# Product-key queries in one pass over four token tiles, or in two passes over pairs with the scatter between them

## The chip, the cores and the metric

One core of a Trainium2 chip runs the whole program. The metric is device microseconds (us) of one execution; lower is better.

## What is computed

One layer: differential attention and an HGRN2 recurrence share an input and an output projection, then a product-key expert layer (PEER) runs on 512 tokens. The change touches the expert layer alone:

```python
def peer_ffn(h, w_query, subkeys, u_table, v_table):      # h: 512 tokens x 1024, blocks of 128
    def one_block(xb):
        q = jnp.einsum('nd,dc->nc', xb, w_query).reshape(PEER_BLOCK, PEER_HEADS, 2, PEER_QUERY_DIM // 2)
        s = jnp.einsum('nhpc,hpkc->nhpk', q, subkeys)       # 8 heads x 2 halves x 128 keys
        sv, si = lax.top_k(s, PEER_TOPK)                    # 16 of 128
        cand_s = sv[:, :, 0, :, None] + sv[:, :, 1, None, :]
        cand_i = si[:, :, 0, :, None] * N_KEYS + si[:, :, 1, None, :]
        top_s, pos = lax.top_k(cand_s, PEER_TOPK)           # 16 of 256 pairs
        experts = jnp.take_along_axis(cand_i, pos, axis=-1)
        gates = jax.nn.softmax(top_s, axis=-1)
        hid = gelu(jnp.einsum('nkd,nd->nk', u_table[experts], xb)) * gates
        return jnp.einsum('nk,nkd->nd', hid, v_table[experts])
```

There are 16384 experts, and each token uses 8 x 16 of them.

## The kernel before

The 512 tokens are four tiles of 128. Three of them (0, 1 and 2, `ND` = 3) are computed densely: for every one of 128 groups of 128 experts, h = gelu(u x) for all 384 tokens, times a table of gates that is zero wherever a token did not choose the expert, then y += h v. The fourth tile (`SP`, tile 3) gathers its own rows of u and v with indirect DMAs.

Products are made of three matmuls each (`mm3`, lines 111 to 113) on a high and a low part of both operands. `split` makes the parts: ScalarE copies the high part (line 107), VectorE or, where `G` is given, GpSimd subtracts it for the low part (line 108). `u_piece` (lines 662 to 668) loads a piece of 128 x 1024 on SP's queue (line 664) and splits it; it has three buffers each for the raw piece `ur` and its parts `uh` and `ul`, which the query weights `wq` share with the pieces of u.

The stages, in the order of the program:

1. Projections, recurrence, attention and the output projection, until 333 us. None of it changes.
2. Queries. A loop over 16 sets (8 heads x 2 halves): 24 matmuls of the set's `wq` with all 512 tokens into `ps_q`, a copy by ScalarE, four matmuls with the keys into `pss` (line 771), then the top 16 of each tile's 128 scores on VectorE (`top16`: two `max`, two `max_index` and a `match_replace`, lines 752 to 756). After every second set GpSimd adds the 54 candidate pairs of a head for four tiles (line 779, five instructions), and VectorE takes the top 16 of each.
3. Softmax of all tiles at once (lines 878 to 895), then `route(0)` (lines 797 to 852), a chain of VectorE operations that turns list positions into expert numbers, then `scatter` (lines 897 to 914): tile 0's gates are added into a zeroed table in HBM (`g_dram[0]`, in the order listings `g_dram_61`) by 8 heads x 16 indirect DMAs from GpSimd (line 904). A head waits until all DMAs of the head before it have landed, since two heads may name the same expert.
4. Gates of tiles 1 and 2. `gates4` (lines 854 to 874) builds one-hot rows `oh` on VectorE, multiplies them on TensorE into `pgt`, and ScalarE copies them to `stg`; SP writes `stg` to `g_dram[1]` and `g_dram[2]` (line 934).
5. Last stage (from line 1008): for each of 128 groups i, SP loads the gates `gsl` (line 1021, after the scatter) and v's piece `vr` (line 1029), and TensorE runs 18 matmuls `y`, then the h piece that refills the ring. GpSimd's gathers for tile 3 (`ug`, line 953) run beside it.

While VectorE and GpSimd route and scatter, TensorE has the h pieces: `run_ahead(n)` takes n steps of the first 40 (`RING`), a piece being 24 matmuls `ps_h` of 384 columns in four steps (`h_parts`, lines 696 to 710). Once 40 are done there is no buffer for another until `y` uses one up; only the loads and splits of piece 40 are issued ahead (`h_load`, line 939), with its low part on GpSimd.

The tile framework's scheduler orders each engine's instructions from the order in the code and its own estimates. GpSimd and SP run in order, so what waits at the head of either holds all behind it.

Of the kernel before, what the change touches and what calls it, by code (L numbers as in the profile page):

```python
# [20 lines left out]
P = 128  # L21
# [40 lines left out]
def tile_kernel(  # L62
# [653 lines left out]
    with ExitStack() as rt:  # L716
        rc = rt.enter_context(tc.tile_pool(name="rc", bufs=1))
        qs = rt.enter_context(ExitStack())
# [31 lines left out]
        def top16(vals, n, vdst, idst):  # L750
            t = rw.tile([P, n], F32, name="t16", tag=f"t16_{n}")
            V.max(vdst[:, 0:8], vals)
            V.max_index(idst[:, 0:8], vdst[:, 0:8], vals)
            V.match_replace(out=t, in_to_replace=vdst[:, 0:8], in_values=vals, imm_value=FMIN)
            V.max(vdst[:, 8:16], t)
            V.max_index(idst[:, 8:16], vdst[:, 8:16], t)

        for s in range(NSET):
            wh, wl = u_piece(wq[s], G) if s else qw_first
            ps = pq.tile([P, SEQ], F32, name="ps_q", tag="pq")  # L760
            parts = [slice(0, 256), slice(256, SEQ)] if s == 0 else [slice(0, SEQ)]
            for part in parts:
                if part.start:
                    s3(SP, X.pop(SP), pg, "pg")
                for kc in range(KC):
                    mm3(ps[:, part], wh[:, kc], wl[:, kc], xbh[:, kc, part], xbl[:, kc, part], kc == 0, kc == KC - 1)
            qT = rw.tile([P, SEQ], F32, name="qT")
            S.activation(qT, ps, AF.Copy)
            pss = pg.tile([P, NTB, NK], F32, name="pss", tag="pg")
            for tb in range(NTB):  # L770
                PE.matmul(pss[:, tb, :], qT[:, tb * P : tb * P + P], skt[:, s, :], start=True, stop=True)
            for tb in range(NTB):
                top16(pss[:, tb, :], NK, SV[tb][:, s, :], SI[tb][:, s, :])
            if s % 2 == 1:
                hh = s // 2
                cand = rw.tile([P, NTB, NCAND], F32, name="cand")
                o = 0
                for a0, na, nb in CBLK:
                    G.tensor_tensor(
                        cand[:, :, o : o + na * nb].rearrange("p t (a b) -> p t a b", b=nb),  # L780
                        SVA[:, :, s - 1, a0 : a0 + na].unsqueeze(3).to_broadcast([P, NTB, na, nb]),
                        SVA[:, :, s, :nb].unsqueeze(2).to_broadcast([P, NTB, na, nb]),
                        op=OP.add,
                    )
                    o += na * nb
                for tb in range(NTB):
                    top16(cand[:, tb], NCAND, TS[tb][:, hh, :], TI[tb][:, hh, :])

        qs.close()
        rw = rt.enter_context(tc.tile_pool(name="rg", bufs=2, reuse_waits="tile"))  # L790
        steps = (None for i in range(RING) for _ in h_parts(i, None, HP))

        def run_ahead(n):
            for _ in range(n):
                next(steps, None)

        def route(tb):
# [3 lines left out]
            def pick(which, sel, op, key, table, dt):  # L801

                eq = rw.tile([P, PH * TOPK, TOPK], dt, name="eq", tag="eq", bufs=1)
# [7 lines left out]
                ix = rw.tile([P, PH, TOPK], U32 if dt == I16 else F32, name=f"ix{which}")  # L811
                V.tensor_tensor(ix.rearrange("p h k -> p (h k)"), eq[:, :, 0], eq[:, :, 1], op=OP.add)
                return ix
# [3 lines left out]
            comb = rw.tile([P, PH, TOPK], I16, name="comb", bufs=1)  # L817
            step = rw.tile([P, PH, TOPK], I16, name="step", bufs=1)
# [6 lines left out]
            k1 = rw.tile([P, PH, TOPK], U32, name="k1", bufs=1)  # L825
            V.tensor_scalar(k1, both, 6, None, op0=OP.logical_shift_right)
            V.tensor_scalar(both, both, 63, None, op0=OP.bitwise_and)
            ixa = rw.tile([P, PH, TOPK], F32, name="ixa")
            V.tensor_copy(ixa, k1)
            rank = rw.tile([P, PH, TOPK], F16, name="rank", bufs=1)  # L830
            V.tensor_tensor(rank, TI[tb], both, op=OP.subtract)
            sif = rw.tile([P, PH, TOPK], F16, name="sif", bufs=1)
# [15 lines left out]
            for i, t in enumerate((idx[0], idx[1], gh[:, tb], TS[tb])):  # L848
                PE.transpose(ptp[:, i, :], t.rearrange("p h k -> p (h k)"), ident)
            pmj = rw.tile([P, 4, P], F16, name="pmj")  # L850
# [25 lines left out]
        run_ahead(16)  # L876

        fl = "p t h k -> p (t h) k"
        mx = rc.tile([P, NTB * PH], F32, name="mx")
        V.tensor_copy(mx, TSA[:, :, :, 0].rearrange("p t h -> p (t h)"))  # L880
        g3 = TSA.rearrange(fl)
        V.tensor_tensor(g3, g3, mx.unsqueeze(2).to_broadcast([P, NTB * PH, TOPK]), op=OP.subtract)
        tc.keep_in_program_order(S.activation(g3, g3, AF.Exp))
        V.tensor_reduce(mx, g3, axis=AX.X, op=OP.add)
        V.reciprocal(mx, mx)
        V.tensor_tensor(g3, g3, mx.unsqueeze(2).to_broadcast([P, NTB * PH, TOPK]), op=OP.mult)
        V.tensor_copy(exp_g, TS[SP].rearrange("p h k -> p (h k)"))
        sc_g = rc.tile([P, PH, TOPK], F32, name="sc_g")
        V.tensor_scalar(sc_g, TS[0], GS, None, op0=OP.mult)
        gh16 = rw.tile([P, ND, PH, TOPK], F16, name="gh16", bufs=1)  # L890
        gh = rw.tile([P, ND, PH, TOPK], F32, name="gh", bufs=1)
        V.tensor_scalar(TSA[:, :ND], TSA[:, :ND], GS, None, op0=OP.mult)
        V.tensor_copy(gh16, TSA[:, :ND])
        V.tensor_copy(gh, gh16)
        V.tensor_tensor(TSA[:, :ND], TSA[:, :ND], gh, op=OP.subtract)

        def scatter(sc_idx):
# [24 lines left out]
        run_ahead(16)  # L922
        acc_ = 0.0
        for tb in range(1, ND):
            pmj = nxt
            for g0 in range(0, P, GB):
# [196 lines left out]
```

## Time and profile before

| | us |
|---|---|
| median of three runs (lowest, highest) | 1693.4 (1690.3, 1697.65) |
| the profiled execution, whole | 1696.98 |
| its span (first to last instruction) | 1695.2 |
| TensorE busy | 1559.5 (92% of the span) |
| VectorE / ScalarE / GpSimd busy | 1197.9 / 642.1 / 683.7 |
| granted TensorE clock, mean | 0.962 |

The profile is of one execution. An engine's busy share is an average over the stages; what bounds a stage is read from that stretch of time: which engine has no idle time there, or what the others wait for. Times in the rows count from the start of the span, which is 1.8 us shorter than the execution's own time.

### The profile page before, as it was taken

The page shows a single profiled execution, that of the slowest core. Times are in us where ns is not written, and L with a number is a line of the kernel's source. Part 1 is how long each engine was busy: PE and PEld are TensorE (multiplying, and loading weights), DVE is VectorE, ACT ScalarE, POOL GpSimd, SP SyncE. Part 2 cuts the span into 40 slices and gives each one's busy share as a digit, 9 for nine tenths or more (in the row PEclk, how much of TensorE's full clock was granted, in tenths as well). Part 3 has the DMA queues.
Part 4 walks back from the last instruction along what each step waited for, and adds up shares of the span by engine and source line. Part 5 has one row for each costly group of instructions (what it writes and reads, how often), then busy time and mean ns, then how long its engine had stood idle before and what let it go on. Part 6 is the DMA issues. An engine that isn't in the chain of part 4 may idle for free.

```text
span 1695.2 us, 23411 instructions
## 1 busy us (share of the span) xinstructions
PE 1559.5 (92%) x8599; PEld 1397.2 (82%) x8599; DVE 1197.9 (71%) x2354; ACT 642.1 (38%) x984; POOL 683.7 (40%) x522
## 2 busy tenths in 40 slices
PE   8999999999699999305999999999999999999997
PEld 7999977788698999204999999999999999998885
DVE  7762667578988877003888777777777787767775
ACT  5223364422256666101333333333333333333333
POOL 3000012334138886874544444444444444433221
PEclk9999999999899999656999999999999999999999
DMA  8511321322144666227999998899899888977883
GB/s 284 190 51 56 108 96 67 131 94 73 57 121 112 199 186 188 1 0 277 342 348 308 321 329 306 306 321 329 307 315 316 321 311 303 337 234 253 285 268 137
DMA packets 166948, 364.00 MB, mean 215 GB/s; under 512 B 31152, under 2 KB 80560, under 8 KB 166704
## 3 DMA queue, kind: packets, MB, share of 16 engines
q1 hardware_dynamic: 110816, 227.11, 38.5%
q0 software_dynamic: 55440, 134.34, 25.4%
q8 instruction: 67, 1.10, 0.2%
q10 hardware_dynamic: 576, 1.05, 0.2%
q14 instruction: 49, 0.40, 0.1%
HBM read 330.92 MB, written 29.43 MB: 213 GB/s over the span
## 4 chain that ended last, share of the span: by engine, by line
PE 70%; POOL 13%; DVE 7%; issue 4%; DMA 3%; ACT 2%; SPq 1%; POOLq 0%; DVEq 0%; ACTq 0%
POOL g_dram L904 12%; PE y L112 10%; PE y L113 10%; PE y L111 10%; PE ps_h L113 7%; PE ps_h L111 7%; PE ps_h L112 7%; DMA g_dram<-sc_g,sc_idx 2%; PE ps_l L351 2%; PE ps_t L113 2%; PE ps_t L111 2%; PE ps_t L112 2%; PE ps_n L111 1%; PE ps_n L112 1%; PE ps_n L113 1%
## 5 line engine op out<-in xcount | busy, mean ns | idle before, releaser
L113 PE MATMUL ps_h<-xbh,ul 128*128 128x384 f32 x1024 | 347.1, 339 | 94.4 <-POOL ul L108 82.1
L111 PE MATMUL ps_h<-xbh,uh 128*128 128x384 f32 x1024 | 350.2, 342 | 1.3 <-ACT hr L707 1.3
L112 PE MATMUL ps_h<-xbl,uh 128*128 128x384 f32 x1024 | 345.8, 338 | 0.0
L111 PE MATMUL y<-vh,wh 128*128 128x512 f32 x768 | 300.2, 391 | 9.9 <-ACT wh L107 9.8
L108 DVE TENSOR_TENSOR vl<-vr,vh 128x1024 fp32r<-128x1024 f32 x128 | 156.8, 1225 | 205.5 <-ACT vh L107 203.8
L112 PE MATMUL y<-vl,wh 128*128 128x512 f32 x768 | 301.6, 393 | 0.0
L113 PE MATMUL y<-vh,wl 128*128 128x512 f32 x768 | 301.6, 393 | 0.0
L967 POOL DMA_INDIRECT vg<-in_v_dram,exp_idx x128 | 186.1, 1454 | 278.0 <-DVE acc L973 208.8
L113 PEld LDWEIGHTS ps_h<-xbh,ul 128*128 128x128 f32 x1024 | 194.2, 190 | 95.8 <-POOL ul L108 82.4
L953 POOL DMA_INDIRECT ug<-in_u_dram,exp_idx x128 | 179.2, 1400 | 216.7 <-DVE jk L957 137.2
L904 POOL DMA_INDIRECT g_dram<-sc_g,sc_idx x128 | 222.4, 1737 | 84.4 <-issue 38.8
L107 ACT ACTIVATE uh<-ur 128x1024 fp32r<-128x1024 f32 x144 | 152.8, 1063 | 267.6 <-PE ps_h L112 175.9
L107 ACT ACTIVATE vh<-vr 128x1024 fp32r<-128x1024 f32 x128 | 136.1, 1063 | 270.4 <-issue 214.8
L111 PEld LDWEIGHTS ps_h<-xbh,uh 128*128 128x128 f32 x1024 | 195.3, 191 | 5.1 <-ACT hr L707 1.5
L112 PEld LDWEIGHTS ps_h<-xbl,uh 128*128 128x128 f32 x1024 | 194.5, 190 | 3.4
L111 PEld LDWEIGHTS y<-vh,wh 128*128 128x128 f32 x768 | 144.9, 189 | 38.9 <-ACT wh L107 10.6
L113 PEld LDWEIGHTS y<-vh,wl 128*128 128x128 f32 x768 | 144.8, 189 | 30.5
L112 PEld LDWEIGHTS y<-vl,wh 128*128 128x128 f32 x768 | 144.8, 189 | 28.6
L973 DVE SCALAR_TENSOR_TENSOR acc<-vg,hid,acc 128x1024 f32<-128x1024 f32 x127 | 162.8, 1282 | 2.1
L108 DVE TENSOR_TENSOR ul<-ur,uh 128x1024 fp32r<-128x1024 f32 x127 | 155.0, 1221 | 7.9 <-ACT uh L107 7.8
L957 DVE SCALAR_TENSOR_TENSOR jk<-ug,xbn 128x1024 f32<-128x1024 f32 x128 | 156.4, 1222 | 4.8 <-DMA ug<-in_u_dram,exp_idx 2.3
L107 ACT ACTIVATE wh<-hr 128x384 fp32r<-128x384 f32 x128 | 67.3, 525 | 226.1 <-DVE hr L1034 226.1
(274 smaller groups left out, 2503.8 us busy)
## 6 DMA issues: line engine op xcount, KB each, us to landing
ur<-in_uT_dram SPq DMA_DIRECT2D x128, 512.0 KB
vr<-in_v_dram SPq DMA_DIRECT2D x128, 512.0 KB
gsl<-g_dram SPq DMA_DIRECT2D x96, 256.0 KB
g_dram<-stg SPq DMA_DIRECT2D x32, 512.0 KB
wr<-in_w_in_dram SPq DMA_DIRECT2D x26, 512.0 KB
g_dram<-zero SPq DMA_DIRECT2D x4, 2048.0 KB
ur<-in_wq_dram SPq DMA_DIRECT2D x16, 512.0 KB
wor<-in_w_out_dram SPq DMA_DIRECT2D x8, 512.0 KB
```

Source lines behind the costliest of these rows:

```text
L107: S.activation(hi, src, AF.Copy)
L108: (eng or V).tensor_tensor(lo, src, hi.bitcast(F32), op=OP.subtract)
L111: PE.matmul(ps, ah, bh, start=first, stop=False)
L112: PE.matmul(ps, ah, bl, start=False, stop=False)
L113: PE.matmul(ps, al, bh, start=False, stop=last)
L351: PE.matmul(ps[:, c, :], KR[h][:, cs], rhs[:, c * P : c * P + P], start=True, stop=True)
L904: ins = G.indirect_dma_start(out=flat, out_offset=bass.IndirectOffsetOnAxis(ap=sc_idx[:, h, k : k + 1], axis=0), in_=sc_g[:, h, k : k + 1] ...
L953: G.indirect_dma_start(out=ug, out_offset=None, in_=u, in_offset=bass.IndirectOffsetOnAxis(ap=exp_idx[:, k : k + 1], axis=0))
L957: V.scalar_tensor_tensor(jk, ug, 1.0, xbn_, op0=OP.mult, op1=OP.mult, accum_out=hid[:, k : k + 1])
L967: G.indirect_dma_start(out=vg, out_offset=None, in_=v, in_offset=bass.IndirectOffsetOnAxis(ap=exp_idx[:, k : k + 1], axis=0))
L973: V.scalar_tensor_tensor(acc, vg, hid[:, k : k + 1], acc, op0=OP.mult, op1=OP.add)
```

## The change

The queries are made in two passes. Pass 1 takes tiles 0 and 1 (matmuls of 256 columns), makes tile 0's lists at once, and puts tile 1's scores by in `sc1` for later. Softmax, route and scatter of tile 0 come next in the code. Pass 2 loads and splits `wq` a second time, with VectorE now in place of GpSimd, and makes the scores of tiles 2 and 3; the lists of tile 1 that were put by, its candidates, softmax and route come in this pass, those of tiles 2 and 3 in the loop over the gates of tile 1. Candidates of tiles 1 to 3 are added on VectorE, eight heads per instruction. Softmax is done per tile, and the scatter reads tile 0's gates from `tsa`, where they are made, in place of a copy `sc_g`. One step of an h piece follows each set of pass 2 in the code, 26 steps stand ahead of the loop over the gates in place of 56, and the rest follows as before.

```diff
+        def scores_of(s, t0, qw):
+            wh, wl = qw
+            ps = pq.tile([P, 2 * P], F32, name="ps_q", tag="pq")
+            part = slice(t0 * P, t0 * P + 2 * P)
+            for kc in range(KC):
+                mm3(ps, wh[:, kc], wl[:, kc], xbh[:, kc, part], xbl[:, kc, part], kc == 0, kc == KC - 1)
+            qT = rw.tile([P, 2 * P], F32, name="qT")
+            S.activation(qT, ps, AF.Copy)
+            pss = pg.tile([P, 2, NK], F32, name="pss", tag="pg")
+            for n in range(2):
+                PE.matmul(pss[:, n, :], qT[:, n * P : n * P + P], skt[:, s, :], start=True, stop=True)
+            return pss
+
+        later = []
+        sc1 = rw.tile([P, NSET, NK], F32, name="sc1", bufs=1)
         for s in range(NSET):
-            wh, wl = u_piece(wq[s], G) if s else qw_first
-            ps = pq.tile([P, SEQ], F32, name="ps_q", tag="pq")
...
-            for tb in range(NTB):
-                top16(pss[:, tb, :], NK, SV[tb][:, s, :], SI[tb][:, s, :])
+            pss = scores_of(s, 0, u_piece(wq[s], G) if s else qw_first)
+            if s == 1:
+                s3(SP, X.pop(SP), pg, "pg")
+            S.activation(sc1[:, s, :], pss[:, 1, :], AF.Copy)
+            top16(pss[:, 0, :], NK, SV[0][:, s, :], SI[0][:, s, :])
             if s % 2 == 1:
                 hh = s // 2
...
+                cand = rr.tile([P, 1, NCAND], F32, name="cand")
+                candidates(G, 0, slice(hh, hh + 1), cand)
+                top16(cand[:, 0], NCAND, TS[0][:, hh, :], TI[0][:, hh, :])
+                if hh:
+                    top16(*later.pop(0))
+            later.append((sc1[:, s, :], NK, SV[1][:, s, :], SI[1][:, s, :]))
...
-                        in_=sc_g[:, h, k : k + 1], in_offset=None, compute_op=OP.add,
+                        in_=TS[0][:, h, k : k + 1], in_offset=None, compute_op=OP.add,
...
+        softmax(0)
+        scattered = scatter(route(0))
+        nxt = None
+        for s in range(NSET):
+            pss = scores_of(s, 2, u_piece(wq[s]))
+            run_ahead(1)
+            for n in range(2):
+                top16(pss[:, n, :], NK, SV[2 + n][:, s, :], SI[2 + n][:, s, :])
+            for _ in range(2):
+                if later:
+                    top16(*later.pop(0))
+            if not later and nxt is None:
+                run_ahead(2)
+                second(1)
+                softmax(1)
+                nxt = route(1)
+                run_ahead(4)
...
         run_ahead(4)
-        scattered = scatter(route(0))
-        run_ahead(8)
-        route(SP)
-        run_ahead(8)
-        nxt = route(1)
-        run_ahead(16)
...
-                if g0 == P // 2 - GB and tb + 1 < ND:
-                    nxt = route(tb + 1)
+                if tb == 1 and g0 < 2 * GB:
+                    t2 = 2 + g0 // GB
+                    second(t2)
+                    softmax(t2)
+                    nxt = route(t2) or nxt
                     run_ahead(2 * HP)
```

`second(tb)` makes the candidates of a tile on VectorE and their top 16; `softmax(tb)` is the old softmax for one tile. `SP` in `softmax` and `route` is the number of the sparse tile, not the engine.

GpSimd's instructions where its candidate sums end and the scatter stands, before (`cand` candidate pairs, `ul` the low part of piece 40, `ug` a gathered row of u):

```order
L779 TENSOR_TENSOR cand<-sva 128x4x10
L779 TENSOR_TENSOR cand<-sva 128x4x12
L779 TENSOR_TENSOR cand<-sva 128x4x8
L779 TENSOR_TENSOR cand<-sva 128x4x16
L904 DMA g_dram_61<-sc_g,sc_idx 2097152x1 x128
L108 TENSOR_TENSOR ul<-ur,uh 128x1024
L953 DMA ug<-in_u_dram,exp_idx 128x1024 x32
```

and with the change:

```order
L766 TENSOR_TENSOR cand<-sva 128x10
L766 TENSOR_TENSOR cand<-sva 128x12
L766 TENSOR_TENSOR cand<-sva 128x8
L766 TENSOR_TENSOR cand<-sva 128x16
L929 DMA g_dram_61<-tsa,sc_idx 2097152x1 x128
L995 DMA ug<-in_u_dram,exp_idx 128x1024 x4
L108 TENSOR_TENSOR ul<-ur,uh 128x1024
L995 DMA ug<-in_u_dram,exp_idx 128x1024 x28
```

The sums are for one tile instead of four, and four gathers moved ahead of the low part of piece 40.

VectorE where tile 0's route ends, before:

```order
L806 TENSOR_TENSOR eq<-eq,io_3439 128x2048
L819 SCALAR_TENSOR_TENSOR comb<-si_3469,starts 128x128
L808 TENSOR_TENSOR eq<-eq,sif 128x2048
L108 TENSOR_TENSOR ul<-ur,uh 128x1024
L810 TENSOR_TENSOR eq<-eq 128x128x8
L833 CAST sif<-si_3471 128x128
L810 TENSOR_TENSOR eq<-eq 128x128x4
L108 TENSOR_TENSOR ul<-ur,uh 128x1024
L810 TENSOR_TENSOR eq<-eq 128x128x2
L812 TENSOR_TENSOR ix_4962<-eq 128x128
L845 SCALAR_TENSOR_TENSOR sc_idx<-ix_4962,off 128x128
```

and with the change (`sva`, `si` values and positions of a list, `t` its second half's input, `sc_3480` tile 1's scores put by):

```order
L830 TENSOR_TENSOR eq<-eq,sif 128x2048
L755 MATCH_REPLACE t_4614<-sva,pss 128x128
L832 TENSOR_TENSOR eq<-eq 128x128x8
L756 MAX sva<-t_4614 128x8
L832 TENSOR_TENSOR eq<-eq 128x128x4
L757 MAX_INDEX si_3474<-sva,t_4614 128x8
L832 TENSOR_TENSOR eq<-eq 128x128x2
L755 MATCH_REPLACE t_4620<-sva,sc_3480 128x128
L834 TENSOR_TENSOR ix_4353<-eq 128x128
L756 MAX sva<-t_4620 128x8
L867 SCALAR_TENSOR_TENSOR sc_idx<-ix_4353,off 128x128
```

Between the operations of the route stand operations of pass 2's lists where splits of h pieces stood.

SP's queue around the first `gsl`, before:

```order
L934 DMA g_dram_63<-stg 128x1024 x4
L664 DMA ur<-in_uT_dram 128x1024 x3
L934 DMA g_dram_63<-stg 128x1024 x4
L1021 DMA gsl<-g_dram_61 128x4x128
L1021 DMA gsl<-g_dram_62 128x4x128
L1021 DMA gsl<-g_dram_63 128x4x128
L1029 DMA vr<-in_v_dram 128x1024 x3
```

and with the change:

```order
L664 DMA ur<-in_uT_dram 128x1024 x3
L973 DMA g_dram_63<-stg 128x1024 x4
L664 DMA ur<-in_uT_dram 128x1024 x2
L1063 DMA gsl<-g_dram_61 128x4x128
L1063 DMA gsl<-g_dram_62 128x4x128
L1063 DMA gsl<-g_dram_63 128x4x128
L1071 DMA vr<-in_v_dram 128x1024 x3
```

The last write of `stg` is no longer between the last loads of u ahead and the first `gsl`.

## Rows read from the trace of the kernel before

**Rows 1.** Page, busy tenths of TensorE in 40 slices of the span.
```profile
PE   8999999999699999305999999999999999999997
```
**Rows 2.** Windows by stage: queries, routes and gates, the hole, first y.
```profile
core 0: us, PE busy (x) PEld busy (x) DVE busy (x) ACT busy (x) POOL busy (x), PEclk, DMA share, GB/s
333.00:490.00 157.00, 143.15 (x738) 123.26 (x737) 133.94 (x823) 46.19 (x58) 43.14 (x76) 0.96 0.25 85
490.00:692.00 202.00, 197.63 (x1293) 186.20 (x1291) 146.44 (x215) 126.40 (x138) 159.77 (x88) 1.00 0.60 154
692.00:773.00 81.00, 0.00 (x0) 0.00 (x0) 0.00 (x0) 0.22 (x1) 64.72 (x42) 0.51 0.20 0
773.00:800.00 27.00, 16.87 (x54) 14.64 (x55) 10.38 (x16) 5.77 (x7) 8.50 (x8) 0.63 0.98 364
```
**Rows 3.** Waits, 686 to 830 us: engine, line <- releaser: us, times, longest.
```profile
PE ps_h L113 <- POOL ul L108: 82.1, 1, 82.1
```
**Rows 4.** Waits of SP's queue, 640 to 830 us.
```profile
SPq L664 <- POOL ul L108: 97.4, 1, 97.4
```
**Rows 5.** Chain of waits: first DMA of heads 1, 3, 4, 6; what follows the scatter.
```profile
490.60 1.74 POOL g_dram L904
...
563.73 1.59 POOL g_dram L904
...
604.81 1.55 POOL g_dram L904
...
677.51 1.99 POOL g_dram L904
...
770.90 2.38 POOL ul L108
```
**Rows 6.** Chain of waits, 686 to 830 us: the first y.
```profile
790.38 0.79 PE y L111
```
**Rows 7.** Timeline of SP's queue, 740 to 800 us: start, duration.
```profile
773.68 3.63 SPq L934 DMA_DIRECT2D g_dram<-stg  x4
777.69 2.94 SPq L1021 DMA_DIRECT2D gsl<-g_dram  x3
```
**Rows 8.** Timeline of TensorE, 333 to 365 us: query matmuls of 256, 512 columns; scores.
```profile
333.44 0.28 PE L112 MATMUL ps_q<-xbl,uh 128*128 128x256 f32 x1
333.56 0.28 PE L113 MATMUL ps_q<-xbh,ul 128*128 128x256 f32 x1
...
341.75 0.40 PE L112 MATMUL ps_q<-xbl,uh 128*128 128x512 f32 x1
341.99 0.40 PE L113 MATMUL ps_q<-xbh,ul 128*128 128x512 f32 x1
...
349.75 1.16 PE L771 MATMUL pss<-skt,qT 128*128 128x128 f32 x8
356.26 1.16 PE L771 MATMUL pss<-skt,qT 128*128 128x128 f32 x8
```
**Rows 9.** Timeline of VectorE: first step of two lists; last list; end of route.
```profile
346.73 0.29 DVE L752 MAX8 sva<-pss 128x8 f32<-128x128 f32 x1
...
347.92 0.29 DVE L752 MAX8 sva<-pss 128x8 f32<-128x128 f32 x1
...
468.49 0.21 DVE L756 FIND_INDEX8 ti<-tsa,t 128x8 uint32<-128x54 f32 x1
...
490.01 0.29 DVE L845 SCALAR_TENSOR_TENSOR sc_idx<-ix,off 128x128 uint32<-128x128 f32 x1
```
**Rows 10.** Timeline of GpSimd, 342 to 356 us: a split, four of five candidate sums.
```profile
343.02 2.38 POOL L108 TENSOR_TENSOR ul<-ur,uh 128x1024 fp32r<-128x1024 f32 x1 [4.50 <-ACT uh L107]
...
354.56 0.90 POOL L779 TENSOR_TENSOR cand<-sva 128x32 f32<-128x32 f32 x4 [2.89 <-DVE sva L752]
```
**Rows 11.** Groups of VectorE, 490 to 692 us: busy, mean ns; idle before.
```profile
L859 DVE TENSOR_TENSOR oh<-io,pmj 128x1024 f16<-128x1024 f16 x64 | 43.7, 689 | 28.0 <-PE pgt L873 26.6 <-issue 1.4
...
L108 DVE TENSOR_TENSOR ul<-ur,uh 128x1024 fp32r<-128x1024 f32 x30 | 36.8, 1226 | 6.1 <-ACT uh L107 6.0
```

More of the change, by code (lines that the diff above doesn't have):

```diff
@@ L717, in tile_kernel @@
         rc = rt.enter_context(tc.tile_pool(name="rc", bufs=1))
+        rr = rt.enter_context(tc.tile_pool(name="rr", bufs=2, reuse_waits="tile"))
         qs = rt.enter_context(ExitStack())
@@ L750, in top16 @@
         def top16(vals, n, vdst, idst):
-            t = rw.tile([P, n], F32, name="t16", tag=f"t16_{n}")
+            t = (rw if n == NK else rr).tile([P, n], F32, name="t16", tag=f"t16_{n}")
             V.max(vdst[:, 0:8], vals)
@@ L756, in top16, with candidates @@
             V.max_index(idst[:, 8:16], vdst[:, 8:16], t)
-        for s in range(NSET):
-            wh, wl = u_piece(wq[s], G) if s else qw_first
-            ps = pq.tile([P, SEQ], F32, name="ps_q", tag="pq")
[L761 to L769, printed above, removed]
-            for tb in range(NTB):
-                PE.matmul(pss[:, tb, :], qT[:, tb * P : tb * P + P], skt[:, s, :], start=True, stop=True)
-            for tb in range(NTB):
-                top16(pss[:, tb, :], NK, SV[tb][:, s, :], SI[tb][:, s, :])
+        def candidates(eng, tb, hs, dst):
+            sv = SVA[:, tb].rearrange("p (h two) k -> p h two k", two=2)
+            n = hs.stop - hs.start
+            o = 0
+            for a0, na, nb in CBLK:
+                full = [P, n, na, nb]
+                eng.tensor_tensor(
+                    dst[:, :, o : o + na * nb].rearrange("p h (a b) -> p h a b", b=nb),
+                    sv[:, hs, 0, a0 : a0 + na].unsqueeze(3).to_broadcast(full),
+                    sv[:, hs, 1, :nb].unsqueeze(2).to_broadcast(full),
+                    op=OP.add,
+                )
+                o += na * nb
@@ new lines, in second @@
+        def second(tb):
+            cand = rr.tile([P, PH, NCAND], F32, name="cand_t", bufs=1)
+            candidates(V, tb, slice(0, PH), cand)
+            for hh in range(PH):
+                top16(cand[:, hh], NCAND, TS[tb][:, hh, :], TI[tb][:, hh, :])
+        def scores_of(s, t0, qw):
[10 more added lines that the diff above has]
+            return pss
@@ L777, in tile_kernel @@
[L777 to L787, printed above, removed]
@@ L801, in pick @@
             def pick(which, sel, op, key, table, dt):
-                eq = rw.tile([P, PH * TOPK, TOPK], dt, name="eq", tag="eq", bufs=1)
+                eq = rr.tile([P, PH * TOPK, TOPK], dt, name="eq", tag="eq", bufs=1)
                 full = [P, PH * TOPK, TOPK]
@@ L874, in gates4, with softmax @@
             S.activation(stg[:, :, c0 : c0 + 4].rearrange("p i t -> p t i"), pgt, AF.Copy)
-        run_ahead(16)
[L878 to L895, printed above, removed]
+        def softmax(tb):
+            g3 = TS[tb]
+            mx = rr.tile([P, PH], F32, name="mx")
+            full = [P, PH, TOPK]
+            V.tensor_copy(mx, g3[:, :, 0])
+            V.tensor_tensor(g3, g3, mx.unsqueeze(2).to_broadcast(full), op=OP.subtract)
+            tc.keep_in_program_order(S.activation(g3, g3, AF.Exp))
+            V.tensor_reduce(mx, g3, axis=AX.X, op=OP.add)
+            V.reciprocal(mx, mx)
+            if tb == SP:
+                V.tensor_tensor(
+                    exp_g.rearrange("p (h k) -> p h k", h=PH), g3, mx.unsqueeze(2).to_broadcast(full), op=OP.mult
+                )
+                return
+            V.tensor_scalar(mx, mx, GS, None, op0=OP.mult)
+            V.tensor_tensor(g3, g3, mx.unsqueeze(2).to_broadcast(full), op=OP.mult)
+            if tb:
+                gh16 = rr.tile([P, PH, TOPK], F16, name="gh16", bufs=1)
+                gh[tb] = rr.tile([P, PH, TOPK], F32, name="gh")
+                V.tensor_copy(gh16, g3)
+                V.tensor_copy(gh[tb], gh16)
+                V.tensor_tensor(g3, g3, gh[tb], op=OP.subtract)
         def scatter(sc_idx):
```

25 lines of the change are left out of this document (12 added, 13 removed).

## The prediction, made before the changed kernel ran

> **What bounds the kernel now.** I read the page's slices first. TensorE is at nine tenths nearly everywhere, but two slices near the middle show 3 and 0 [rows 1]. The windows by stage put the hole at 692 to 773 us: TensorE does nothing in those 81 us, VectorE nothing, and only GpSimd works, 64.7 us [rows 2]. The waits of that stretch name it: one wait of 82.1 us of a `ps_h` matmul for a low part `ul` from GpSimd [rows 3]; SP's queue stood still for 97.4 us for the same split [rows 4]. That split is not slow. The chain of waits shows it to begin at 770.90, the moment the scatter's last instruction is through, and the scatter's first DMA is at 490.60 [rows 5]. So GpSimd sends scatter DMAs for 280.3 us, the first `gsl` loads come behind that, and the first `y` is at 790.38 [rows 6]. TensorE has the first 40 h pieces as cover and they are used up at 692. From the first `y` on TensorE is busy to the end [rows 1], so the time moves one for one with the first `y`, less what TensorE did before it.
>
> What sets the start of the scatter? The last list of candidates ends at 468.5 and the route's last operation at 490.0 [rows 9], so the route takes 21.8 us. The lists end at 468.5 because all four tiles' scores and lists are made first: 16 sets of 6.51 us each on TensorE [rows 8] and 64 + 32 lists on VectorE, which is busy for 133.9 of that window's 157 us [rows 2].
>
> **The change, part by part.** *Start of the scatter.* Pass 1 is 16 sets of 24 matmuls of 256 columns, 0.12 us apart, and half of the 1.16 us of score matmuls [rows 8]: 16 x (2.88 + 0.58) = 55.4 us. From 333.4 and with some 2 us for the last tile's transposes and the few h matmuls between, the last scores stand at 391. Per pair of sets (6.9 us of TensorE) VectorE now has two lists of 1.19 us [rows 9], one of candidates of about two thirds of that, and from the second head on one put-by list: 4.4 us and some splits. GpSimd has two splits of 2.38 us and five sums at no more than a quarter of 0.90 to 0.90 each, for a quarter of the columns [rows 10]: 6.0 us at the most. Both are under TensorE's 6.9, so TensorE sets the pace. After the last scores come a copy, a list, the sums, a list of candidates and two or three splits of 1.23 us [rows 11], 8 us in all: 399. The route is the same chain and takes its 21.8 us; the list operations that now stand in it (the order listing) replace splits of 1.2 us and are 0.3 us each. The scatter starts at **421** instead of 490.6. Bounds: 410 if the route runs at the pace of its own operations without others between, 450 if some six sets' worth of pass 2's lists get in front.
>
> *Length of the scatter.* Five heads ran beside other work, (677.5 - 490.6) / 5 = 37.4 us each, the last three in the hole, (770.9 - 677.5) / 3 = 31.1 us each; the longest was 604.8 - 563.7 = 41.1 [rows 5]. Now the other engines work beside nearly all of it. What runs beside the first heads has changed, from one-hot rows (0.69 us each, half of VectorE's time) to lists and splits, and no row shows a head beside those; the bounds are the quiet head, 8 x 31.1 = 249 us, and the longest, 8 x 41.1 = 329 us. I take seven loaded and one quiet, 293 us, because the early heads lie beside query work, which moved data in a DMA share of 0.25 instead of 0.60 [rows 2]. End: 421 + 293 = **714** instead of 770.9.
>
> *From the end of the scatter to the first y.* That took 790.4 - 770.9 = 19.5 us. In it SP wrote the last `stg` and only then issued `gsl`: 773.7 to 777.7, 4.0 us [rows 7]. With the change no `stg` write waits there (the order listing), so 15.5 us: first `y` at 729.5, which is 60.9 earlier. Against that, piece 40's 24 matmuls ran in the hole before and now follow the first `y`; 384 columns lie midway between 0.12 and 0.22 us ((6.51 - 1.16) / 24 for 512 columns [rows 8]), so 24 x 0.17 = 4.1 us are given back. Gain: 56.8 us.
>
> *What is added, at no cost.* Query matmuls: 48 of 0.12 instead of 24 of 0.22 us per set, 0.4 us more, 6.5 us over 16 sets. TensorE's work up to the end of the ring was 143.2 + 197.6 = 340.8 of 359 us [rows 2]; its ring would end at 699 instead of 692, and y waits until 729.5 anyway: the cover is 30 us. Here a rule speaks against the change. The trace has 256 columns at 0.12 us and 512 at 0.22 [rows 8], that is nearly in proportion. The Trainium skill (TensorE: Matmul & The Clock Gate, Back-to-back issue gap) says that the spacing of sustained matmuls is set by weight load and matmul together, 81 ns at 128 columns and 131 ns at 512, so that halving the columns does not halve the time; an estimate from that page, by interpolation, is 98 ns at 256 and 25 us more for TensorE instead of 6.5. The trace disagrees on both figures, and even 25 us would lie inside the cover.
>
> VectorE: 16 more splits of 1.23 us [rows 11], 19.6 us; 15 wide candidate sums and three more sets of small softmax steps, some 10 us. It had 280.4 us of work in 359 [rows 2], and has 310 in about 370. Bound: hidden as long as TensorE has h pieces to do meanwhile; the rival below has the price if not. ScalarE copies 16 more high parts and 16 score tiles, with 172.6 us busy of 359 [rows 2]: hidden. SP loads 16 more pieces of 512 KB while the DMA share is 0.25 to 0.60 [rows 2]: hidden. On GpSimd four gathers go ahead of piece 40's split; nothing before the first `y` waits for that split now. The copy `sc_g` goes: under a microsecond on VectorE.
>
> **Sum.** 790.4 - 729.5 - 4.1 = 56.8. The profiled execution took 1697.0, so 1640.2 for it; it stood 3.6 above the median of 1693.4, so **1637** against the median.
>
> **The rivals.**
>
> *VectorE makes TensorE late (1659).* In pass 2 each set gives VectorE four lists (two of its own, two put by) and one split of `wq`, 4 x 1.19 + 1.23 = 6.0 us, and a quarter of an h piece, 0.3; TensorE has 3.46 + 1.0. Sixteen sets at 6.3 instead of 4.5 us leave TensorE 29 us behind, and tile 1's candidates, softmax and route, on which the first `gates4` waits, another 20 us. The ring would end at 699 + 29 + 20 = 748, the first `y` come at 752 and the gain be 34 us: 1659. For it: the raw and split pieces have three buffers each for `wq` and h, and the one-hot groups already show 28.0 us of VectorE idle around `pgt` [rows 11]. Against it: the scheduler may put other h steps in those gaps, and the order listing has them there. By the page named above this would be some 18 us later still.
>
> *The scatter starts late (1666).* If pass 2's lists, which become ready in the middle of the route, push it to 450, the scatter ends at 743, the first `y` is at 758.5 and the gain 27.8 us. For: the lists stand between the route's steps. Against: they are 0.2 to 0.3 us each [rows 9].
>
> *Slower: the heads stretch (1711).* The scatter is sent by GpSimd, an instruction per 128 values, and each head waits for the last. With VectorE busy beside all eight, in a mixture of operations that no head has run beside, a head could take longer than the 41.1 us seen. With heads of 46 us the scatter ends at 421 + 368 = 789, the first `y` is at 804.5, and with the 4.1 us it is 18 us worse: 1711. It decides from (790.4 - 4.1 - 15.5 - 421) / 8 = 43.7 us a head. For: loaded heads are 20% longer than quiet ones [rows 5]. Against: five loaded heads together were 37.4. The Trainium skill (SBUF — State Buffer, SBUF: two separate sides) has a rule for this: descriptors of DMAs sent from GpSimd's queue are written by GpSimd, which cannot reach the port it shares with VectorE while VectorE runs an operation in a two-port mode. The trace agrees in direction (37.4 against 31.1); which VectorE operation costs how much no row shows.
>
> *The change does nothing* (within 0.5%): the scatter starts no earlier because something else in front of it waits, or heads fall between 42.7 and 44.8 us. No row speaks for the first.
>
> **How the numbers follow.** Half a percent is 8.5 us, about what a measurement of this kernel can tell from no change. The forecast has 0.72; its own bounds are a quiet scatter, where TensorE's ring (699) becomes the limit and the time some 1610, and heads all of 41.1 us, which end at 750 and give 1673. TensorE late has 0.15, the late start 0.08, slower 0.04, nothing 0.01. The range from 1612 to 1668 holds most of the forecast and the middles of the two milder rivals; outside are slower, nothing, and the far ends. Faster by over 0.5%: 0.72 + 0.15 + 0.08 less 0.02 for heads near 43 us, 0.93; same 0.03; slower 0.04.
>
> **What would show it.** Right: the first scatter DMA between 410 and 430; heads of 34 to 39 us; the hole in TensorE at most 40 us long and ending near 730; `gsl` issued directly when the scatter's DMAs have landed. Wrong: a first `y` later than the scatter's end by over 20 us with TensorE still on `ps_h` or `pgt` (VectorE made it late); a first DMA after 440; heads above 42 us. If the first `y` is where I put it and the time is not, then the stage after it lost what was gained, which no row of before would have told.

## The result, and the profile after

The changed kernel took 1652.4 us (median of four runs, 1646.9 to 1656.0) against 1692.1 us: the ratio is 0.976 with a 95% interval of 0.972 to 0.979, some 40 us faster. The forecast was 1637 with 1612 to 1668 as its range.

The profiled execution took 1646.9 us, the fastest of the four. Its slices of TensorE still show a dip where two slices stood at 3 and 0 [rows 1], but only one of them:

```profile
PE   7999998989599999939999999999999999999997
```

The windows by stage, in the same columns as [rows 2], here for most of pass 1, its end with the route, pass 2, the gates, and the hole that is left (VectorE's one-hot rows begin at 508, in the third):

```profile
333.00:391.00 58.00, 53.49 (x410) 50.67 (x410) 37.61 (x224) 25.10 (x47) 38.05 (x66) 0.97 0.40 139
391.00:420.00 29.00, 22.40 (x157) 20.78 (x156) 28.87 (x138) 15.62 (x20) 2.00 (x11) 0.94 0.24 86
420.00:555.00 135.00, 122.99 (x819) 116.82 (x820) 126.89 (x526) 64.79 (x78) 110.34 (x61) 0.94 0.54 126
555.00:710.00 155.00, 153.35 (x1004) 144.62 (x1001) 105.44 (x202) 93.61 (x103) 121.04 (x63) 1.00 0.62 174
710.00:737.00 27.00, 0.01 (x1) 0.01 (x1) 1.72 (x3) 3.91 (x6) 14.15 (x11) 0.56 0.63 191
```

TensorE is at work in pass 1 (53.5 of 58 us) and nearly full in the gates stage (153.4 of 155), VectorE is full from 391 to 420 us (28.9 of 29) and nearly so in pass 2, and the hole is 27 us instead of 81. What stands in it is told by GpSimd's timeline. The first line is the start of the scatter, the next two the worst DMA of it and the one behind, the last two its end and the first gather:

```profile
419.78 1.74 POOL L929 DMA_INDIRECT g_dram<-tsa,sc_idx  x1 [18.96 <-DVE sc_idx L867]
...
583.21 13.32 POOL L929 DMA_INDIRECT g_dram<-tsa,sc_idx  x1 [0.30 <-issue]
596.84 1.55 POOL L929 DMA_INDIRECT g_dram<-tsa,sc_idx  x1 [0.30 <-issue]
...
717.92 1.55 POOL L929 DMA_INDIRECT g_dram<-tsa,sc_idx  x1 [0.30 <-issue]
719.78 1.02 POOL L995 DMA_INDIRECT ug<-in_u_dram,exp_idx  x1 [0.30 <-issue]
```

The scatter starts at 419.8 instead of 490.6 [rows 5] and takes 300.0 us to the instruction behind it instead of 280.3. Its heads, from first DMA to first DMA, take 34.4, 37.9, 34.2 and 38.4 us in pass 2, 50.9, 35.6 and 37.1 in the gates stage, and 31.5 at the end. TensorE's own timeline shows the last matmul of the ring and the first `y`:

```profile
709.47 0.34 PE L113 MATMUL ps_h<-xbh,ul 128*128 128x384 f32 x1
...
737.00 0.79 PE L111 MATMUL y<-vh,wh 128*128 128x512 f32 x1 [27.19 <-ACT wh L107]
```

The first `y` comes at 737.0 instead of 790.4 [rows 6]. Between it and the scatter's end the chain of waits (start, duration, what) reads:

```profile
717.92 3.00 DMA g_dram<-tsa,sc_idx
...
721.04 0.39 SPq L1063
...
722.57 0.50 SPq L1071
...
723.78 10.53 DMA vr<-in_v_dram
```

The first `gsl` load is issued at 721.04, as soon as the last scatter DMA is down, with no write of `stg` in between as there was in [rows 7]; but v's piece then takes 10.5 us to land.

### The profile page after: what moved, and what is told of

Same layout as the page of the kernel before. It is cut to its first block, busy times and chain, and to the rows that moved or that the text cites. A ratio compares the mean times of both kernels' runs of the same rounds, so it can differ in the third digit from the quotient of the medians.

```text
span 1645.1 us, 24305 instructions
## 1 busy us (share of the span) xinstructions
PE 1565.9 (95%) x8959; PEld 1416.4 (86%) x8959; DVE 1216.9 (74%) x2403; ACT 671.2 (41%) x1040; POOL 696.0 (42%) x522
## 4 chain that ended last, share of the span: by engine, by line
PE 54%; DMA 1%; ACT 0%; DVE 0%; issue 0%; SPq 0%; POOL 0%; DVEq 0%; POOLq 0%; ACTq 0%
PE y L112 11%; PE y L113 11%; PE y L111 11%; PE ps_h L113 7%; PE ps_h L111 7%; PE ps_h L112 7%; DMA vr<-in_v_dram 1%; DMA g_dram<-tsa,sc_idx 0%; DVE hx L1037 0%; DVE hx L1045 0%; ACT jk L1038 0%; SPq L1063 0%; SPq L1071 0%; ACT vh L107 0%; ACT uh L107 0%
## 5 line engine op out<-in xcount | busy, mean ns | idle before, releaser
L929 POOL DMA_INDIRECT g_dram<-tsa,sc_idx x128 | 239.5, 1871 | 79.1 <-issue 40.3
L107 ACT ACTIVATE uh<-ur 128x1024 fp32r<-128x1024 f32 x160 | 169.8, 1062 | 141.3 <-PE ps_h L112 73.7
L108 DVE TENSOR_TENSOR ul<-ur,uh 128x1024 fp32r<-128x1024 f32 x143 | 174.2, 1219 | 22.1 <-ACT uh L107 18.8
```

The lines of the kernel that those rows point to most:

```text
L107: S.activation(hi, src, AF.Copy)
L108: (eng or V).tensor_tensor(lo, src, hi.bitcast(F32), op=OP.subtract)
L929: ins = G.indirect_dma_start(out=flat, out_offset=bass.IndirectOffsetOnAxis(ap=sc_idx[:, h, k : k + 1], axis=0), in_=TS[0][:, h, k : k + 1 ...
```

## Experiments

Ratios are to the kernel before, with their 95% intervals; the changed kernel stands at 0.976 [0.972, 0.979].

**The scatter behind both passes.** If the two passes, the softmax by tile or the order on SP's queue were worth something by themselves, it would show with the scatter put back.

```diff
-        softmax(0)
-        scattered = scatter(route(0))
         nxt = None
         for s in range(NSET):
...
+        softmax(0)
+        scattered = scatter(route(0))
         qs.close()
```

> Both passes as in the change, but tile 0's softmax, route and scatter stand behind pass 2 in the code. Theory (the time follows the first y, and that the scatter's end): pass 2's last lists stood at about 505 us in the changed kernel's trace and the route takes some 20, so the scatter starts at 500 to 525, lasts 8 x 37 = 296 us, and the first y comes 17 us later, at 813 to 838, later than the 790 of the kernel before: 1710 to 1740 us. Rival (the gain comes from splitting the queries, the softmax by tile or the order on SP's queue, wherever the scatter stands): 1650 to 1690 us.

Measured: 1725.1 us, ratio 1.021 [1.019, 1.023]. GpSimd's and TensorE's timelines have the scatter's first DMA and the first `y`:

```profile
507.57 11.21 POOL L929 DMA_INDIRECT g_dram<-tsa,sc_idx  x1 [105.75 <-DVE sc_idx L867]
```
```profile
813.83 0.79 PE L111 MATMUL y<-vh,wh 128*128 128x512 f32 x1 [106.30 <-ACT wh L107]
```

The rest of the change without the early scatter is a loss of 2%: GpSimd stands idle for 105.75 us until the route's last result is there, and the first `y` is 23 us later than before the change.

**One pass, tile 0's lists first.** Matmuls of 512 columns as before, scores of tiles 1 to 3 put by, and the rest as in the change.

```diff
-            pss = scores_of(s, 0, u_piece(wq[s], G) if s else qw_first)
+            wh, wl = u_piece(wq[s], G) if s else qw_first
+            ps = pq.tile([P, SEQ], F32, name="ps_q", tag="pq")
...
-            S.activation(sc1[:, s, :], pss[:, 1, :], AF.Copy)
+            S.activation(sc1[:, s], pss[:, 1:], AF.Copy)
```

> One pass of queries over all four tiles as before the change (512 columns), but tile 0's lists at once, the scores of tiles 1 to 3 put by, and tile 0's softmax, route and scatter ahead of their lists. Theory (TensorE's 6.5 us per set of four tiles hold the scatter back, so both the order of the lists and the halved queries are needed): last scores at 333 + 16 x 6.5 = 438 plus 2, scatter from about 469 (20 us earlier than before, 49 later than with the change), six loaded and two quiet heads, 289 us, first y at 775, less the 4 us of piece 40: 1675 to 1690 us. Rival (putting the other tiles' lists off does all of it): scatter from about 425 and 1645 to 1660 us.

Measured: 1683.6 us, ratio 0.996 [0.994, 0.998]. The scatter starts at 467.05, takes 288.8 us, and the first `y` is at 772.0. So putting off the other tiles' lists gives some 8 of the 40 us; the rest needs TensorE to make tile 0's scores in half the time.

**Half of the heads.** What stands behind the scatter?

```diff
-            for h in range(PH):
+            for h in range(PH // 2):
```

> The changed kernel with the scatter of heads 0 to 3 alone; the gates of heads 4 to 7 of tile 0 are left out. Theory (behind the scatter TensorE's own work stands 27 us lower, and the last stage takes what it gets): the scatter ends at about 570, TensorE goes from the ring's end at 710 straight to y, and the time is 25 to 32 us below the changed kernel: 1620 to 1630 us. Rival 1 (the last stage is held by its DMAs or by GpSimd's gathers, not by when it starts): within 10 us of 1652. Rival 2 (nothing else is near, the scatter alone counts): 100 us or more faster.

Measured: 1623.2 us, ratio 0.960 [0.959, 0.962]. TensorE goes from the ring to `y` with 3.62 us between:

```profile
709.38 0.34 PE L113 MATMUL ps_h<-xbh,ul 128*128 128x384 f32 x1
713.34 0.80 PE L111 MATMUL y<-vh,wh 128*128 128x512 f32 x1 [3.62 <-ACT wh L107]
```

The scatter was over at 567.5. Taking 152 us off it brings 29 us and no more: the ring's end at 709 is the next limit. Had gathers or DMAs of the last stage held it, these 29 us would not have come.

**The scatter in two halves.** The same limit, reached with the whole computation: heads 0 to 3 are routed and scattered after eight sets of pass 1.

```diff
+EARLY = 4
...
-            pss = scores_of(s, 0, u_piece(wq[s], G) if s else qw_first)
+            pss = scores_of(s, 0, (u_piece(wq[s], G if s < EARLY * 2 else None) if s else qw_first))
...
-                candidates(G, 0, slice(hh, hh + 1), cand)
+                candidates(G if hh < EARLY else V, 0, slice(hh, hh + 1), cand)
...
+                if hh == EARLY - 1:
+                    softmax(0, slice(0, EARLY))
+                    scattered = scatter(route(0, slice(0, EARLY)), slice(0, EARLY))
...
-        softmax(0)
-        scattered = scatter(route(0))
+        softmax(0, slice(EARLY, PH))
+        scattered = scatter(route(0, slice(EARLY, PH)), slice(EARLY, PH), scattered)
```

> The changed kernel with tile 0's softmax, route and scatter in two halves: heads 0 to 3 after the first eight sets of pass 1, heads 4 to 7 after pass 1; the splits and candidate sums of the later sets of pass 1 go from GpSimd to VectorE. Theory (one for one with the scatter's start, until TensorE's ring end is the limit): lists of head 3 at about 371, half a route in 15 us, scatter from about 388 instead of 420, end at 688, first y when TensorE has done its ring at 710 to 718: 15 to 27 us below the changed kernel, 1625 to 1637 us. Rival (VectorE, which now has eight more splits and a second route in pass 1, makes TensorE late by as much as the scatter gains): 1645 to 1660 us.

Measured: **1624.6 us**, ratio 0.961 [0.959, 0.963], the best whole version of the study; one other equals it. The scatter's first DMA, and TensorE from the ring to `y`:

```profile
385.42 1.74 POOL L914 DMA_INDIRECT g_dram<-tsa,sc_idx  x1 [13.92 <-DVE sc_idx L853]
```
```profile
711.57 0.34 PE L114 MATMUL ps_h<-xbh,ul 128*128 128x384 f32 x1
716.51 0.79 PE L112 MATMUL y<-vh,wh 128*128 128x512 f32 x1 [4.60 <-ACT wh L108]
```

It takes the scatter away from the limit: 34 us earlier, over at 690.9, and the time falls by 28, just past the 15 to 27 that I expected. VectorE's eight more splits cost TensorE's ring 2 us (711.6 instead of 709.5), so the rival falls.

**Fewer one-hot rows.** The long DMA instructions stand in the gates stage, beside VectorE's one-hot work.

```diff
+            if c0 == 0:
+                ohs.append(rw.tile([P, 4, P, 4], F16, name="oh", bufs=3))
+            oh = ohs[-1]
...
+            if c0 == 0:
                 V.tensor_tensor(
                     oh[:, :2],
```

> The changed kernel with the one-hot rows of a group of 32 tokens built for its first four only and used for all 32: seven of eight one-hot operations on VectorE are left out (the gates of tiles 1 and 2 are then those of other tokens). Theory 1 (VectorE's operations on two SBUF operands hold back GpSimd's sending of scatter DMAs): the stalls of 4 to 13 us go, heads in the gates stage take 31 to 34 us instead of 50.9, 35.6 and 37.1, the scatter takes 275 to 285 us instead of 300, and the time is 1625 to 1637 us. Theory 2 (traffic of the DMA queues lengthens the heads): heads stay at 35 us and more, the time within 5 us of the changed kernel.

Measured: 1628.1 us, ratio 0.961 [0.958, 0.964]. Heads 5 to 7 take 34.1, 33.6 and 33.0 us, no DMA instruction lasts over 4 us, and the scatter is over at 695.0 instead of 719.5. The group of the scatter's last 64 DMAs in the changed kernel (564 to 719 us), and in this one (564 to 695 us); the columns are those of [rows 11]:

```profile
L929 POOL DMA_INDIRECT g_dram<-tsa,sc_idx x64 | 124.2, 1941 | 34.6 <-issue 22.3 <-DMA g_dram<-tsa,sc_idx 12.2
```
```profile
L934 POOL DMA_INDIRECT g_dram<-tsa,sc_idx x64 | 102.8, 1606 | 31.2 <-issue 21.6 <-DMA g_dram<-tsa,sc_idx 9.6
```

Most of the difference is in the instructions themselves, 21 us over 64 of them, and little in the waits for the heads before.

**The one-hot rows from PSUM.** Is it the amount of VectorE's work or its kind? Here all one-hot operations stay, and one operand of each is read from PSUM.

```diff
-            pmj = rr.tile([P, 4, P], F16, name="pmj")
-            S.activation(pmj, ptp, AF.Copy)
-            return pmj
+            return ptp
```

> The changed kernel with the transposed gates and positions (pmj) left in PSUM as float32, where the one-hot operations of VectorE read them, instead of copied to SBUF as float16: all one-hot operations stay, but each has one operand in SBUF and one in PSUM instead of two in SBUF (and PSUM has two buffers fewer for the other tiles). Theory 1a (two SBUF operands of VectorE's one-hot operations hold the DMA instructions back): no DMA instruction of the scatter over 5 us in the gates stage, heads 5 to 7 at 31 to 36 us. Theory 1b (any unbroken stretch of one-hot work on VectorE does): stalls of 6 to 13 us stay. The time itself says little, as the one-hot operations may take longer with float32 from PSUM.

Measured: 1668.4 us, two runs, ratio 0.988 [0.984, 0.991]. VectorE is busier than in the changed kernel from 555 to 710 us, 139.5 of the 155 us instead of 105.4, and a one-hot operation takes 1.21 us instead of 0.69:

```profile
555.00:710.00 155.00, 142.83 (x882) 133.61 (x881) 139.49 (x204) 82.21 (x92) 116.41 (x67) 0.93 0.57 144
```
```profile
L886 DVE TENSOR_TENSOR oh<-oh,ptp 128x1024 f16<-128x1024 f16 x40 | 48.4, 1212 | 0.2
```

VectorE's timeline shows a gap before 552.26 and none from there until the one before 623.42:

```profile
552.26 1.22 DVE L829 TENSOR_TENSOR eq<-eq,io 128x2048 f16<-128x2048 f16 x1 [0.43 <-ACT eq L828]
...
623.42 1.23 DVE L108 TENSOR_TENSOR ul<-ur,uh 128x1024 fp32r<-128x1024 f32 x1 [2.44 <-ACT uh L107]
```

Yet no DMA instruction of the scatter is over 3.4 us, heads 5 to 7 take 36.1, 33.6 and 36.5 us, and the scatter is over at 700.9. The group of its last 64 DMAs (564 to 701 us):

```profile
L928 POOL DMA_INDIRECT g_dram<-tsa,sc_idx x64 | 111.4, 1740 | 28.6 <-issue 22.6 <-DMA g_dram<-tsa,sc_idx 6.0
```

So it is not how much VectorE works, nor that it works without a gap, here for 68 us. It is the one-hot operations with both operands in SBUF; whether by where the operand lies or by its type and the faster rate, this run doesn't separate, since both changed. The time is long for another reason, VectorE holding TensorE up, as in a rival of the prediction, though in another stage: the chain of waits goes through the one-hot operations, TensorE's one-hot matmuls end at 745.5, and the first `y` comes at 761.6.

```profile
743.09 1.23 DVE oh L886
744.37 0.30 PE pgt L893
745.51 1.03 ACT stg L895
...
761.60 0.79 PE y L111
```

**A table per head.** Heads 1 to 7 go to tables of their own, and no head waits for another.

```diff
-                        out=flat, out_offset=bass.IndirectOffsetOnAxis(ap=sc_idx[:, h, k : k + 1], axis=0),
+                        out=flats[h], out_offset=bass.IndirectOffsetOnAxis(ap=sc_idx[:, h, k : k + 1], axis=0),
...
-                    for b in before:
-                        tc.add_manual_dep(ins, b.name, SYNC, reason="the head before may have the same expert")
```

> The changed kernel with heads 1 to 7 of the scatter going to tables of their own, so that no head waits for the one before it (the gates of these heads are left out of the table that is read). Theory (the wait at a head's end is part of its length): the seven waits of the changed kernel's trace, 2.4, 3.2, 1.6, 4.0, 4.3, 3.6 and 4.4 us, sum to 23.5 and fall to 0.3 each: scatter 21 us shorter, 277 to 282 us, time 1628 to 1640 us. Rival (the sending of the DMAs is held back elsewhere instead, by a queue that fills): scatter 290 us or more, time within 8 us of the changed kernel.

Measured: 1632.3 us, ratio 0.963 [0.960, 0.967]; the scatter takes 284.4 us, 16 less than in the changed kernel's first profile and 23 less than in its second (below). The scatter is 2 us longer than expected, but the theory holds: the waits at the heads' ends are a part of the scatter. The stall of 13 us stays (13.35 us at 582.27), and so does one of 6.9 at 548, which the second profile has too and the first has not; so the 23 us are the closer comparison.

**v's pieces ahead of the gates loads.**

```diff
+        for i in range(2):
+            vrs.append(dp.tile([P, D], F32, name="vr", tag="vr", bufs=3))
+            nc.sync.dma_start(vrs[-1], v[i * P : i * P + P, :])
         for i in range(NK):
```

> The changed kernel with the first two loads of v's pieces ahead of the first gates loads on SP's queue. Theory (v's pieces, which need nothing of the scatter, wait behind the gates and land 10.4 us after issue beside them and four gathers; they end the chain to the first y): from the scatter's end to the first y 9 to 13 us instead of 17.2, time 4 to 8 us below the changed kernel. Rival (the gates loads themselves take as long): 15 us or more, time within 3 us.

Measured: 1646.0 us, ratio 0.971 [0.968, 0.974]. From the scatter's end, where the first gather is sent (723.5), to the first `y` (737.2) it is 13.7 us instead of 17.2: less than I expected, because the gates loads then end the chain, as its lines show:

```profile
725.98 9.91 DMA gsl<-g_dram
...
736.02 0.57 DVE hr L1083
...
736.61 0.53 ACT wh L107
...
737.19 0.79 PE y L111
```

The interval meets the changed kernel's, so 6 us by the medians is more than this run can claim; the 3.5 us of the profile is what it shows. Both moves together, the halved scatter and v's pieces first:

> The scatter in two halves (as in early_half) and the first two loads of v's pieces ahead of the first gates loads (as in vr_first). Theory (TensorE's ring end at 712 is the limit and 4.6 us between it and the first y are left, of which v's pieces cost a part): 1 to 4 us below early_half, 1620 to 1624 us. Rival (the gates loads set the first y as well): 1624 to 1628 us.

Measured: 1624.6 us, ratio 0.962 [0.961, 0.963]. Nothing is gained over the halved scatter alone; the first `y` is at 716.4 instead of 716.5, and the rival holds: on the chain of waits a load of gates ends last.

```profile
701.60 13.51 DMA gsl<-g_dram
```

**The changed kernel once more.**

> The changed kernel once more. Theory (its spread of 9 us from run to run, against 4 where the scatter does not bound, is the scatter's own): its profile shows a scatter of another length than 300 us, with the stalls elsewhere, and its time differs from the first profile's by the same difference. Rival: the scatter takes 300 us again, and a difference in time arises in another stage.

Measured: 1652.5 us (1644.0 to 1655.9), ratio 0.973 [0.969, 0.978]. This profile, of an execution of 1655.9 us, has the stall of 13 us in its old place and one more:

```profile
548.83 6.87 POOL L929 DMA_INDIRECT g_dram<-tsa,sc_idx  x1 [0.30 <-issue]
...
583.20 13.34 POOL L929 DMA_INDIRECT g_dram<-tsa,sc_idx  x1 [0.30 <-issue]
```
```profile
744.83 0.80 PE L111 MATMUL y<-vh,wh 128*128 128x512 f32 x1 [34.88 <-ACT wh L107]
```

The scatter takes 307.5 us instead of 300.0, the first `y` is 7.8 us later, the execution 9.0. I had expected the stalls elsewhere; the large one is in the same place, and what differs is whether the one at 549 occurs. In the first profile VectorE had the same operations there, begun within 0.03 us of these times, and the DMA instruction was short:

```profile
548.84 1.58 POOL L929 DMA_INDIRECT g_dram<-tsa,sc_idx  x1 [0.30 <-issue]
```

The five other kernels whose scatter starts by 421 us and that build all one-hot rows from SBUF (half of the heads, the halved scatter, a table per head, v's pieces first, both moves) have one of 6.9 to 7.1 us there as well: the first profile is the exception. Where the scatter doesn't bound, the runs lie closer: 1623.1 to 1627.2 for the halved scatter, 1622.7 to 1625.1 for half of the heads.

## Why the prediction was right, and what it missed

**The bound.** The forecast rested on one sentence: the time moves one for one with the first `y`. The profiled executions bear it out. Time less first `y` is 909.9 and 911.0 us in the two profiles of the changed kernel, 910.5 with the late scatter, 910.1 in one pass, 911.8 with half of the heads, 910.7 with the halved scatter. Before the change it was 1697.0 - 790.4 = 906.6; the 4.1 us for piece 40's matmuls make 910.7. First `y` ranges from 713 to 814 us in these, and the rest of the program takes the same within 2 us; it is 909.8 to 911.6 with fewer one-hot rows, a table per head, v's pieces first and both moves. With the one-hot rows from PSUM it is 1668.2 - 761.6 = 906.6: there, as before the change, piece 40's matmuls are done ahead of the first `y`, which bears the 4.1 us out.

**Start of the scatter.** 419.8 for a forecast of 421, but in part by luck. The last scores of pass 1, the last step of the last list of candidates, and the route's last operation:

```profile
397.96 0.71 PE L792 MATMUL pss<-skt,qT 128*128 128x128 f32 x4
```
```profile
403.16 0.21 DVE L757 FIND_INDEX8 ti<-tsa,t 128x8 uint32<-128x54 f32 x1
...
419.21 0.27 DVE L867 SCALAR_TENSOR_TENSOR sc_idx<-ix,off 128x128 uint32<-128x128 f32 x1
```

Pass 1's pace was TensorE's, as I said, but at 3.61 us a set where 3.46 were priced, and TensorE stood still for 4.05 us ahead of the first scores. The last scores came at 398 instead of 391, and the last list ended at 403.4 instead of 399. The route then took 16.3 us instead of 21.8, counted as in the prediction; what made it shorter no run takes apart. The two errors cancel. The late rival (450) didn't come.

**Length of the scatter: the term that was mis-sized.** I took "seven loaded and one quiet, 293 us"; it was 300.0 in one profile and 307.5 in the other. In the first profile the pass-2 heads were as priced, 34 to 38 us; in the second the fourth of them took 46.0. The step that failed was to take the loaded heads of before as one kind: the excess is where one-hot rows are made, and in single instructions, 13.3 us in both profiles and 6.9 more in one. The head with the 13.3 us took 50.9 and 48.6 us, over the 42 that the prediction had named as a sign of being wrong. Before the change the longest in the gates stage was this, on the chain of waits:

```profile
575.09 6.10 POOL g_dram L904
```

VectorE's timeline in the changed kernel, beside the DMA instruction that began at 583.21:

```profile
585.59 1.23 DVE L108 TENSOR_TENSOR ul<-ur,uh 128x1024 fp32r<-128x1024 f32 x1
586.73 1.30 DVE L881 TENSOR_TENSOR oh<-io,pmj 128x1024 f16<-128x1024 f16 x2
587.93 1.30 DVE L887 TENSOR_TENSOR oh<-oh,pmj 128x1024 f16<-128x1024 f16 x2
589.13 1.23 DVE L108 TENSOR_TENSOR ul<-ur,uh 128x1024 fp32r<-128x1024 f32 x1
...
595.14 0.69 DVE L881 TENSOR_TENSOR oh<-io,pmj 128x1024 f16<-128x1024 f16 x1
596.26 0.69 DVE L881 TENSOR_TENSOR oh<-io,pmj 128x1024 f16<-128x1024 f16 x1 [0.43 <-PE pgt L895]
```

From 583 on one-hot operations, the last operations of a route (until 585) and splits follow each other without a gap. The first gap that the timeline shows is the 0.43 us before 596.26, and the DMA instruction ends at 583.21 + 13.32 = 596.5. In the halved scatter and with the late scatter the long instructions likewise lie beside operations of this kind. Fewer one-hot rows made them go, and so did an operand in PSUM: that they need VectorE's one-hot operations on SBUF operands is shown, by one profile each, against an instruction of 4.7 to 14.0 us begun between 575 and 586 us in all nine that scatter there with these operations in full. What ends one is open. It looks like the gap here, but the one of 6.87 us ends at 555.7 among list operations that follow without a gap, and one of the halved scatter ends at 594.16 in the middle of one-hot work:

```profile
584.97 9.19 POOL L914 DMA_INDIRECT g_dram<-tsa,sc_idx  x1 [0.30 <-issue]
```
```profile
593.25 1.29 DVE L873 TENSOR_TENSOR oh<-oh,pmj 128x1024 f16<-128x1024 f16 x2
594.45 0.73 DVE L867 TENSOR_TENSOR oh<-io,pmj 128x1024 f16<-128x1024 f16 x1
```

What starts one is open too, as the short instruction at 548.84 shows.

The prediction weighed a rule here: the Trainium skill (SBUF — State Buffer, SBUF: two separate sides) names VectorE's two-port modes as what keeps GpSimd from writing descriptors. The Trainium skill (SBUF — State Buffer, Who interferes with whom) counts `tensor_tensor` as having no such mode, says that with both inputs in SBUF it contends with GpSimd's reads, and infers that it leaves the writing of descriptors alone. From 585.6 on the operations beside the 13.3 us are all `tensor_tensor`, so by the first of these statements the two-port modes are not what held this one; that the long instructions went with one input in PSUM agrees with the second statement. These DMA instructions read their positions `sc_idx` in SBUF as well; whether that reading or the writing of descriptors is held up, no run here shows.

So the slower rival was right that VectorE's work can stretch a head; it needed heads of 43.7 us on the average to decide, and had one or two of eight at 46 to 51.

**From the scatter's end to y.** Forecast 15.5, measured 17.2 (719.8 to 737.0) and 17.5 (727.3 to 744.8). The 4.0 us of `stg` writes went as priced; v's piece took 10.5 us to land where it had taken 6.3 before. Loads of gates, v and u and four gathered rows now start within 5 us; that they slow each other is likely, but no run takes them apart.

**What was put at nothing.** TensorE's ring ended at 709.8, not 699. Some 5 of the 10.8 us are sets of 3.61 us where 3.46 were priced (32 x 0.15), and 5 are waits for splits on VectorE: 17.7 us from 333 us on, where it had waited 12.4 before the change. The cover of 30 us held it. The rival that VectorE makes TensorE late (1659) had put 49 us here, by a count that was too high: pass 1 already makes seven of tile 1's sixteen lists, so nine are left for pass 2 and not two for each of its sixteen sets. That is 16 x (2 x 1.19 + 1.23 + 0.3) + 9 x 1.19 = 73 us on VectorE against TensorE's 16 x 4.46 = 71. A delay by VectorE came only with one-hot operations of 1.21 us, in the gates stage, at 1668. Halved columns cost what the row said: sets of 3.61 us, of which 0.71 are scores, so 2.90 us for 24 matmuls, against 6.51 - 1.16 = 5.35 for 512 columns, a ratio of 0.54. The two figures of the Trainium skill (TensorE: Matmul & The Clock Gate, Back-to-back issue gap) gave about 0.75 by the estimate of 98 and 131 ns; the trace disagrees with it.

**The sum.** Against the first profile the forecast was 1640.2 and the execution took 1646.9: 7.0 us of scatter and 1.7 of loads too little, 1.2 of start and 0.8 of the rest too much. Against the median it was 15 us off, as I subtracted 3.6 for where the profile before stood among its runs, and the first profile after was itself the fastest of four; the second, at 1655.9, is 15.7 above the sum, 14.5 of it scatter. The executions of a kernel whose time hangs on the scatter differ by its stalls, and the difference of one profile from a median isn't carried over to the next kernel.

## What to carry to other kernels

Find the instant from which the bounding engine runs to the end without a hole, and price a change by that instant alone: what starts the chain ahead of it, how long its parts take, and what stands next behind it. A chain of small indirect DMAs from GpSimd is started as soon as its own first part of the data is there, even in pieces, and its price per DMA is taken from the same kind of VectorE work that will run beside it, not from an average of all. When the chain has left the limit (here the two halves: 1624.6 us, at TensorE's ring end), more work on it brings nothing.

## What was not expected of the hardware

A DMA instruction on GpSimd that takes 1.55 us when undisturbed took 13.3 us at the same place in four profiles of kernels with this gates loop (9.2 and 14.0 in the two with the halved scatter), beside an unbroken run of VectorE operations on two SBUF operands. With more VectorE work, 68 us of it without a gap, but one operand of the one-hot operations in PSUM, the longest was 3.4 us. The price of that on VectorE was 1.21 us for an operation of 1024 elements per partition that took 0.69 with both operands as float16 in SBUF.
